# A 2x2 average pool whose first two tiles are loaded on two DMA queues

## The chip, the cores and the metric

The kernel runs on one core of a Trainium2 chip. The metric is the time of one execution on the device in microseconds (us), and where several runs were made, their median. The profile's span, from the first to the last of the program's instructions, is about 1.8 us shorter than that time.

## The reference, cut to what matters

```python
# x: (32, 128, 256, 256) float32; kernel_size = stride = 2; output (32, 128, 128, 128)
for i in range(h_out):
    for j in range(w_out):
        window = x[:, :, 2*i:2*i + 2, 2*j:2*j + 2]
        output[:, :, i, j] = np.mean(window, axis=(2, 3))
```

Each output is the mean of four inputs. 1073.74 MB come in, 268.44 MB go out, and there are three additions and a multiplication for each output.

## The kernel before

The work is cut into 128 tiles. A tile is 128 partitions with 32 units each, and a unit is two rows of an image (2 KB in, 512 B out). The first 127 tiles are alike; the last is loaded in parts of 16, 8 and 8 units, so that the end of the program can be handled in smaller pieces. There are two input buffers of 64 KB and three result buffers of 16 KB in each partition. SyncE issues the loads, VectorE adds rows and then columns, ScalarE multiplies by 0.25 and issues the stores.

```python
def tile_sums(b):                        # VectorE
    take(dve, stored[b], 16)             # the store of two tiles ago has left the result buffer
    take(dve, loaded[b], 16)             # the tile is there
    sums(ins[b], res[b], 2)              # rows, then columns in two halves

def scale_store(t, b, landed):           # ScalarE
    tile_scale(b, scaled)                # two halves; before the second one: free[b] += 1
    take(act, scaled, 2)
    act.dma_start(out=ot[t], in_=res[b]).then_inc(landed, 16)

load(0, 0)                               # SyncE: 8.389 MB each
load(1, 1)
# ... then for each tile t: take(sp, free[b]); load(t, b); at the end the three parts, and
for k, t in enumerate((whole - 2, whole - 1)):
    take(sp, held[k], 2)                 # the stores of the last two whole tiles go out
    sp.dma_start(out=ot[t], in_=res[t % 2]).then_inc(tail, 16)   # behind the last loads

# ScalarE: tile 0 apart from the loop, the others in it; the last two whole tiles:
for k, t in enumerate((whole - 2, whole - 1)):
    tile_scale(t % 2, held[k], frees=k == 0)
```

`take` waits for a semaphore and takes the amount off again. `held` tells SyncE that a result is ready for one of the last stores.

Of the kernel before, what the change touches and what calls it, by code (L numbers as in the profile page):

```python
# [9 lines left out]
@with_exitstack  # L10
def kernel(
    ctx: ExitStack,
    tc: tile.TileContext,
    x: bass.AP,
    kernel_size: bass.AP,
    stride: bass.AP,
    out: bass.AP,
):
    nc = tc.nc
    P = nc.NUM_PARTITIONS  # L20

    n, c, h, w = x.shape
    k = int(kernel_size)
    s = int(stride)
    h_out = (h - k) // s + 1
    w_out = (w - k) // s + 1
    R = n * c * h_out
    units = R // P if R % P == 0 else 0


    if k == 2 and s == 2 and h % 2 == 0 and w == 256 and units >= 1024:
        _pool_2x2(ctx, tc, x, out, units)
    else:
        _generic_pool(ctx, tc, x, out, k, s, n, c, h, w, h_out, w_out)


TILE = 32


def _pool_2x2(ctx, tc, x, out, units):  # L40
    nc = tc.nc
    P = nc.NUM_PARTITIONS
    f32 = mybir.dt.float32
    w = x.shape[3]
    w_out = w // 2
    sp, act, dve = nc.sync, nc.scalar, nc.vector

    xv = x.rearrange("n c (ho a) w -> (n c ho) (a w)", a=2)
    ov = out.rearrange("n c ho wo -> (n c ho) wo")


    in_pool = ctx.enter_context(tc.tile_pool(name="inp", bufs=2))
    out_pool = ctx.enter_context(tc.tile_pool(name="outp", bufs=3))
    ins = [in_pool.tile([P, TILE, 2 * w], f32, name="in_tile") for _ in range(2)]
    res = [out_pool.tile([P, TILE, w_out], f32, name="res") for _ in range(3)]

    def sem(name):
        return ctx.enter_context(nc.semaphore(name))

    loaded, free, stored = [[sem(f"{n}{b}") for b in range(2)] for n in ("loaded", "free", "stored")]  # L60
    halfway, summed, scaled, tail = [sem(n) for n in ("halfway", "summed", "scaled", "tail")]
    held = [sem(f"held{k}") for k in range(2)]



    def take(engine, sem, n=1):
        engine.wait_ge(sem, n)
        engine.sem_inc(sem, -n)  # L68

    def block(r0, g):  # L70
        rows = slice(r0, r0 + g * P)
        return xv[rows].rearrange("(p g) f -> p g f", p=P), ov[rows].rearrange("(p g) f -> p g f", p=P)

    whole, rest = divmod(units - 1, TILE)
    rest += 1
    xt = xv[0:whole * TILE * P].rearrange("(t p g) f -> t p g f", p=P, g=TILE)
    ot = ov[0:whole * TILE * P].rearrange("(t p g) f -> t p g f", p=P, g=TILE)
    parts, a = [], 0
    while a < rest:
        b = rest if rest - a <= 8 else a + (rest - a) // 2  # L80
        parts.append((a, b, sem(f"part{len(parts)}")))
        a = b



    def halves(pieces=2):
        if pieces == 1:
            return [slice(None)]
        return [slice(0, TILE // 2), slice(TILE // 2, TILE)]

    def load(t, b):
        sp.dma_start(out=ins[b], in_=xt[t]).then_inc(loaded[b], 16)

    def sums(it, dst, pieces=1):
        dve.tensor_add(out=it[:, :, 0:w], in0=it[:, :, 0:w], in1=it[:, :, w:]).then_inc(halfway)  # L95
        take(dve, halfway)
        for g in halves(pieces):
            dve.tensor_add(out=dst[:, g], in0=it[:, g, 0:w:2], in1=it[:, g, 1:w:2]).then_inc(summed)  # L98

    def tile_sums(b):  # L100
        take(dve, stored[b], 16)
        take(dve, loaded[b], 16)
        sums(ins[b], res[b], 2)

    def scale(dst, done=scaled):
        act.mul(out=dst, in_=dst, mul=0.25).then_inc(done)  # L106

    def tile_scale(b, done, frees=True):
        for k, g in enumerate(halves()):
            take(act, summed)  # L110
            if k and frees:
                act.sem_inc(free[b])
            scale(res[b][:, g], done)

    def scale_store(t, b, landed):
        tile_scale(b, scaled)
        take(act, scaled, 2)
        act.dma_start(out=ot[t], in_=res[b]).then_inc(landed, 16)

    with tc.tile_critical():  # L120

        load(0, 0)
        load(1, 1)
        pairs = (whole - 2) // 2
        with sp.Fori(2, 2 + 2 * pairs, 2) as i:
            for b in range(2):
                take(sp, free[b])
                load(i + b, b)
        for t in range(2 + 2 * pairs, whole):
            take(sp, free[t % 2])  # L130
            load(t, t % 2)



        take(sp, free[whole % 2])
        it, dst = ins[whole % 2], res[2]
        for a, b, part in parts:
            sp.dma_start(out=it[:, a:b], in_=block((whole * TILE + a) * P, b - a)[0]).then_inc(part, 16)
        for k, t in enumerate((whole - 2, whole - 1)):
            take(sp, held[k], 2)  # L140
            sp.dma_start(out=ot[t], in_=res[t % 2]).then_inc(tail, 16)


        for b in range(2):
            dve.sem_inc(stored[b], 16)
        with dve.Fori(0, whole // 2):
            for b in range(2):
                tile_sums(b)
        if whole % 2:
            tile_sums(0)  # L150
        for a, b, part in parts:
            take(dve, part, 16)
            sums(it[:, a:b], dst[:, a:b])


        scale_store(0, 0, stored[0])
        pairs = (whole - 3) // 2
        with act.Fori(1, 1 + 2 * pairs, 2) as i:
            for b in (1, 0):
                scale_store(i + 1 - b, b, stored[b])  # L160
        for t in range(1 + 2 * pairs, whole - 2):
            scale_store(t, t % 2, stored[t % 2])
        for k, t in enumerate((whole - 2, whole - 1)):
            tile_scale(t % 2, held[k], frees=k == 0)
        for a, b, _ in parts:
            take(act, summed)
            scale(dst[:, a:b])
            take(act, scaled)
            act.dma_start(out=block((whole * TILE + a) * P, b - a)[1], in_=dst[:, a:b]).then_inc(tail, 16)


    with tc.tile_critical():
        take(sp, tail, 16 * (len(parts) + 2))
# [95 lines left out]
```

## Time and profile before

| | before |
|---|---|
| median, lowest, highest (3 runs) | 3102.14, 3102.13, 3103.87 us |
| span of the profiled run | 3100.3 us |
| VectorE busy, ScalarE busy | 54%, 16% |
| load queue q1 and store queue q10, share of 16 DMA engines | 80.3%, 19.9% |
| moved over the span | 1342.19 MB, 433 GB/s |

The two shares of the DMA queues add up to the whole span, so the 16 DMA engines are the resource that is used up. The prediction shows the lines and reads them.

### The profile page before, as it was taken

To read this page: it belongs to the slowest core of one execution; us is meant where nothing else is said; L and a number is where in the kernel's file an instruction comes from. 1 tells how busy PE (TensorE), PEld (TensorE's weight loads), DVE (VectorE), ACT (ScalarE), POOL (GpSimd) and SP (SyncE) were. 2 spreads that over 40 slices of the span, in tenths; PEclk is the share of its full clock that TensorE was granted. 3 is DMA by queue.
4 is the path that set the end of the run, shared out by engine and by line. 5 is a ranking of instruction groups with operands and counts; after the bars stand their busy time and mean duration, and the time that the engine had idled before them with its cause. 6 is when DMAs were issued, how large, how long until landed. Compare 5 with 4: busy or idle time off the path is not lost. (4 is left out here: it accounts for less than half of the span.)

```text
span 3100.3 us, 2993 instructions
## 1 busy us (share of the span) xinstructions
DVE 1688.1 (54%) x387; ACT 490.3 (16%) x258; POOL 0.2 (0%) x4
## 2 busy tenths in 40 slices
DVE  4555555555555555555555555555555555555556
ACT  1111111111111111111111111111111111111111
POOL 0000000000000000000000000000000000000000
DMA  9999999999999999999999999999999999999999
GB/s 418 438 438 424 440 431 431 440 426 436 440 426 437 440 423 439 438 424 440 428 435 440 426 436 440 426 437 440 423 440 438 424 440 427 435 440 426 436 440 413
DMA packets 37440, 1342.19 MB, mean 433 GB/s; under 512 B 4160, under 2 KB 4160, under 8 KB 4416
## 3 DMA queue, kind: packets, MB, share of 16 engines
q1 hardware_dynamic: 19008, 1077.94, 80.3%
q10 hardware_dynamic: 18432, 264.25, 19.9%
HBM read 1073.74 MB, written 268.44 MB: 433 GB/s over the span
## 5 line engine op out<-in xcount | busy, mean ns | idle before, releaser
L95 DVE TENSOR_TENSOR in_tile<-in_tile 128x8192 f32<-128x8192 f32 (+1 forms) x130 | 1112.9, 8561 | 1385.7 <-DVEq L68 1385.7
L106 ACT ACTIVATE res<-res 128x2048 f32<-128x2048 f32 (+1 forms) x257 | 489.0, 1903 | 2569.5 <-ACTq L68 2569.5
L98 DVE TENSOR_TENSOR res<-in_tile 128x2048 f32<-128x2048 f32 (+1 forms) x257 | 575.4, 2280 | 19.0
L106 ACT ACT_TABLE_LOAD x1 | 1.3, 1283 | 34.3 <-ACTq L68 34.3
L250 POOL MEMSET const-bfloat16-1.0<- 128x1 bf16 x1 | 0.1, 101 | 0.0
L250 POOL MEMSET const-uint8-127<- 128x1 uint8 x1 | 0.1, 101 | 0.0
L250 POOL MEMSET const-float32-0.0<- 128x1 f32 x1 | 0.1, 98 | 0.2 <-issue 0.2
L250 POOL MEMSET const-float32-1.0<- 128x1 f32 x1 | 0.1, 98 | 0.0
## 6 DMA issues: line engine op xcount, KB each, us to landing
out_dram<-res ACTq DMA_DIRECT2D x125, 2048.0 KB, 32.5
in_tile<-in_x_dram SPq DMA_DIRECT2D x1, 4096.0 KB, 19.9
in_tile<-in_x_dram SPq DMA_DIRECT2D x2, 2048.0 KB, 26.6
out_dram<-res SPq DMA_DIRECT2D x2, 2048.0 KB, 23.7
in_tile<-in_x_dram SPq DMA_DIRECT2D x127, 34.3
out_dram<-res ACTq DMA_DIRECT2D x1, 1024.0 KB, 9.0
out_dram<-res ACTq DMA_DIRECT2D x2, 512.0 KB, 6.3
```

Of the source, the lines that this page charges most:

```text
L95: dve.tensor_add(out=it[:, :, 0:w], in0=it[:, :, 0:w], in1=it[:, :, w:]).then_inc(halfway)
L98: dve.tensor_add(out=dst[:, g], in0=it[:, g, 0:w:2], in1=it[:, g, 1:w:2]).then_inc(summed)
L106: act.mul(out=dst, in_=dst, mul=0.25).then_inc(done)
L250: nc = _bacc.Bacc("TRN2", target_bir_lowering=False, num_devices=1)
```

## The change

The intent is to start both queues at once. In the trace of the kernel before, the store queue has nothing to do until the first store is issued at 39.42 us, so it takes a quarter of each of the first two tiles. GpSimd joins the two halves of a load into the one semaphore that VectorE waits for. A dummy activation is to bring the load of ScalarE's table forward, which comes at 34.31 us in that trace. Two smaller edits come along: the last two whole tiles are scaled in one piece instead of two halves, and the first tile is now in ScalarE's loop.

```diff
+SIDE = 8
...
-    held = [sem(f"held{k}") for k in range(2)]
+    held, begun = [[sem(f"{n}{k}") for k in range(2)] for n in ("held", "begun")]
...
-        load(0, 0)
-        load(1, 1)
+        for b in range(2):
+            for engine, g in ((sp, slice(0, TILE - SIDE)), (act, slice(TILE - SIDE, TILE))):
+                engine.dma_start(out=ins[b][:, g], in_=xt[b][:, g]).then_inc(begun[b], 16)
+            take(nc.gpsimd, begun[b], 32)
+            nc.gpsimd.sem_inc(loaded[b], 16)
...
-            take(sp, held[k], 2)
+            take(sp, held[k])
...
-        scale_store(0, 0, stored[0])
-        pairs = (whole - 3) // 2
-        with act.Fori(1, 1 + 2 * pairs, 2) as i:
+        act.mul(out=scratch, in_=nc.const_aps.tensor(0.0, [P, 1], f32), mul=0.25)
+        pairs = (whole - 2) // 2
+        with act.Fori(0, 2 * pairs, 2) as i:
...
-            tile_scale(t % 2, held[k], frees=k == 0)
+            take(act, summed, 2)
+            if k == 0:
+                act.sem_inc(free[t % 2])
+            scale(res[t % 2], held[k])
```

More of the change, by code (lines that the diff above doesn't have):

```diff
@@ L55, in _pool_2x2 @@
     res = [out_pool.tile([P, TILE, w_out], f32, name="res") for _ in range(3)]
+    scratch = ctx.enter_context(tc.tile_pool(name="scratch", bufs=1)).tile([P, 1], f32, name="scratch")
     def sem(name):
@@ L106, in scale, with scale_store @@
         act.mul(out=dst, in_=dst, mul=0.25).then_inc(done)
-    def tile_scale(b, done, frees=True):
+    def scale_store(t, b, landed):
         for k, g in enumerate(halves()):
             take(act, summed)
-            if k and frees:
+            if k:
                 act.sem_inc(free[b])
-            scale(res[b][:, g], done)
-    def scale_store(t, b, landed):
-        tile_scale(b, scaled)
+            scale(res[b][:, g])
         take(act, scaled, 2)
@@ L153, in _pool_2x2 @@
             sums(it[:, a:b], dst[:, a:b])
-        scale_store(0, 0, stored[0])
-        pairs = (whole - 3) // 2
-        with act.Fori(1, 1 + 2 * pairs, 2) as i:
-            for b in (1, 0):
-                scale_store(i + 1 - b, b, stored[b])
-        for t in range(1 + 2 * pairs, whole - 2):
+        act.mul(out=scratch, in_=nc.const_aps.tensor(0.0, [P, 1], f32), mul=0.25)
+        pairs = (whole - 2) // 2
+        with act.Fori(0, 2 * pairs, 2) as i:
+            for b in range(2):
+                scale_store(i + b, b, stored[b])
+        for t in range(2 * pairs, whole - 2):
             scale_store(t, t % 2, stored[t % 2])
         for k, t in enumerate((whole - 2, whole - 1)):
-            tile_scale(t % 2, held[k], frees=k == 0)
+            take(act, summed, 2)
+            if k == 0:
+                act.sem_inc(free[t % 2])
+            scale(res[t % 2], held[k])
         for a, b, _ in parts:
```

## The prediction

> **What bounds the kernel now.** I read the page of the kernel before in this order: the busy time of the engines, the slices with their DMA shares, the DMA queues. Then I asked the trace for stretches of ten tiles in the middle, for the timeline at both ends and for the waits.
>
> ```profile
> span 3100.3 us, 2993 instructions
> DVE 1688.1 (54%) x387; ACT 490.3 (16%) x258; POOL 0.2 (0%) x4
> DMA  9999999999999999999999999999999999999999
> q1 hardware_dynamic: 19008, 1077.94, 80.3%
> q10 hardware_dynamic: 18432, 264.25, 19.9%
> HBM read 1073.74 MB, written 268.44 MB: 433 GB/s over the span
> ```
>
> The busiest compute engine works 54% of the span, while the packets of the two DMA queues (q1 is the load queue of SyncE, q10 the store queue of ScalarE) fill 80.3% + 19.9% = 100.2% of the time of the 16 DMA engines. So the bound is the transfer of 1342.19 MB, and the question for any change is: does it remove bytes (this one does not), does it raise the rate, or does it remove time in which the engines have no packet? The middle gives the rate. In the windows of the middle the columns are DVE, ACT and POOL busy, the TensorE clock (unused here), the DMA share and GB/s.
>
> ```profile
> 300.00:542.00 242.00, 131.86 (x30) 38.39 (x21) 0.00 (x0) 1.00 1.00 433
> 2000.00:2242.00 242.00, 131.85 (x30) 38.20 (x20) 0.00 (x0) 1.00 1.00 434
> ```
>
> Ten tiles take 242 us and the DMA share is 1.00. More exactly, the timeline starts the first sum of tile 3 at 91.31 us and that of tile 125 at 3041.47 us, so one tile takes (3041.47 - 91.31) / 122 = 24.18 us. A tile is 8.389 MB in and 2.097 MB out, 10.486 MB, which makes 433.6 GB/s. The packet records of the trace fit: an engine moves one partition's 64 KB in 2.418 us and one partition's 16 KB of a store in 0.605 us, and eight of each per tile make 8 x 3.023 = 24.18 us. The program is 128 such tiles (127 and a last one in three parts): 128 x 24.18 = **3095.2 us** at the steady rate. That leaves 3100.3 - 3095.2 = 5.1 us for everything the change could touch at the two ends. The timeline shows where they are.
>
> ```profile
> 0.95 0.87 SPq L92 DMA_DIRECT2D in_tile<-in_x_dram  x2
> 23.07 8.69 DVE L95 TENSOR_TENSOR in_tile<-in_tile 128x8192 f32<-128x8192 f32 x1 [23.07 <-DVEq L68]
> 34.31 1.28 ACT L106 ACT_TABLE_LOAD   x1 [34.31 <-ACTq L68]
> 36.80 0.34 SPq L92 DMA_DIRECT2D in_tile<-in_x_dram  x1
> 39.42 0.39 ACTq L118 DMA_DIRECT2D out_dram<-res  x1
> 42.41 8.69 DVE L95 TENSOR_TENSOR in_tile<-in_tile 128x8192 f32<-128x8192 f32 x1 [6.00 <-DVEq L68]
> 3094.17 0.34 ACTq L169 DMA_DIRECT2D out_dram<-res  x1
> ```
>
> The first packet starts at 2.02 us and the last ends at 3098.99 us in the packet records, a stretch of 3096.97 us. So the 5.1 us split into 2.02 us before the first packet, 3096.97 - 3095.2 = 1.8 us of imperfect filling in between, and 1.3 us after the last packet (its completion and the closing barrier). Counting the packets in flight, I find 16 of 16 engines holding a packet in every half microsecond from 3.0 to about 3098, including the two places where one would look for a hole: around 41 us, between the second load and the third, and from 3065 us on, where the last parts are summed. What the eye takes for a loss at the start (DVE idle for 23 us, then 6.00 us before the second tile) is idle time of an engine that is not the bottleneck. It costs nothing: the second tile landed 42.41 - 23.07 = 19.34 us after the first, and 8.389 MB in 19.34 us is 433.7 GB/s, so **one queue alone already ran at the full rate**.
>
> [...] loads alone from one queue ran at 433.7 GB/s, loads and stores from two at 433.6 GB/s. [...] The trace shows that alternation from the first store on: one 64 KB packet, one 16 KB packet. [...]
>
> **The change part by part.**
>
> 1. *Splitting the first two loads.* Each tile was 8 packets of 64 KB on each engine; it becomes 8 of 48 KB from the load queue and 8 of 16 KB from the store queue. The bytes are the same: 8 x (1.814 + 0.605) = 8 x 2.418 = 19.35 us, with the 48 KB packet taken as three quarters of the measured 64 KB one. If the two queues take turns, tile 0 still lands near 22.9 us and tile 1 19.35 us later. The store queue is otherwise empty until 39.42 us, so nothing is displaced. Gain or loss on the path: 0. The four issues cost ScalarE some 0.4 us each (0.393 and 0.425 us on SyncE), beside an idle engine. Both issuers leave the opening barrier at about 0.8 us, so the first packet still starts near 2.0 us. The fill of the first packets (they took 3.1 to 3.4 us in place of 2.42, about 0.7 us) stays, for it is the first latency of each engine whatever the queue.
>
> 2. *The relay through GpSimd.* It waits for both halves and adds to the semaphore that VectorE waits on. A hop of that kind (ScalarE's wait, its increment, SyncE's wait met) runs from 36.49 to 36.60 us in this trace, so 0.1 to 0.2 us more on tile 0 and tile 1, and then nothing. It lies beside the transfer of tile 1, thus 0 on the end.
>
> 3. *The dummy activation.* It moves the 1.28 us table load from 34.31 us to about 2 us, where ScalarE is idle. The scale of the first half begins 1.28 us earlier; the second half still waits for its sum (about 36.5 us) and starts near 36.6 in place of 37.4, so the first store is issued about 0.9 us earlier, at some 38.5 us. The engines are still moving tile 1 until 41.4 us, so the store only joins the queue earlier. Stores begin up to one round (0.6 us of transfer per engine) sooner, and the loads then land that much later: an exchange inside a saturated stream, 0 on the end.
>
> 4. *The third load* is issued when tile 0's second sum is picked up, 36.80 us, against an end of tile 1 at 41.4 us. Even with the relay's 0.2 us, the queue is fed about 4 us ahead. In steady state the next load is issued about 13.7 us after a tile lands, with 24.18 us of work, of which about 10 us are left in the queue.
>
> 5. *The last two whole tiles scale in one piece.* One activation of 4096 elements: two halves took 1.91 us each, so I estimate 3.7 us, starting when both sums are there. The held store of tile 125 moves from 3056.99 to about 3058.8 us, that of tile 126 from 3081.1 to about 3082.9 us. Both go to the end of a load queue that holds earlier work: the store of tile 125 landed 32.6 us after its issue, at 3089.6 us, so the one behind it needs to be in the queue only by about 3088. Cost 0. The first part's scale starts at 3085.87 us, after the longer activation is over.
>
> 6. *The tail.* The last store is issued at 3094.17 us and needs about 1.2 us of transfer at 433 GB/s, yet the engines work until 3098.99: there are about 2.5 us of backlog to absorb a VectorE chain that comes later by the 0.6 us of part 3.
>
> Sum: 0 on the rate, 0 on the bytes, between -1 and +0.5 us at the ends. I take -0.3 us, mostly for the third load's first packets, which took 2.5 to 2.8 us and may come back to 2.42 once the store's start no longer falls on them.
>
> **The rivals.** *(a) The two-queue start fills the engines better.* If the first latencies of two queues overlap, the 0.7 us of fill shrinks, and with it perhaps the bubble of the third load. For it: the two together are most of the 1.8 us. Against it: both queues run on the same 16 engines[...]. It would make 3100.5 to 3101.2 us. *(b) A new hole.* ScalarE's issues come late, tile 0's last 16 KB pieces wait behind 48 KB packets of tile 1, and the third load comes after tile 1 has ended. One such packet is 1.8 us, the feed is 4 us ahead, so two would be needed before anything shows: 3102 to 3105 us. *(c) A shifted tail.* The later held stores or the later VectorE chain outrun the 2.5 us of backlog: 3102.5 to 3104 us. *(d) The phase of the two queues changes for good,* and 127 tiles each gain or lose. [...] a loss would need a queue to run dry each round, against 10 us of lead. I hold it for very unlikely.
>
> **Range and chances.** The time before is 3102.14 us with one run of three at 3103.87, a spread of 1.7 us that is larger than the effect. I predict 3101.8 us. Rival (a) sets the lower end at 3100.2; rivals (b) and (c) and the chance that the median falls on the higher value set the upper end at 3103.9. Two per cent are 62 us, twelve times all the time that is not steady transfer, so within 2% is all but certain: 0.985, faster 0.005, slower 0.01.
>
> **What would show it right or wrong.** In the profile after: the middle windows still at 242 us per ten tiles; VectorE's first start at 22.9 to 23.4 us and its second 19.3 to 19.5 us later (a first start above 24.5 speaks for (b)); the table load before 3 us and the first store issued near 38.5 us; a last store issue between 3093.5 and 3095.5 us with packets still in flight for some 4 us after it. A change of span above 2 us with the same middle would say that an end holds a hole I have not seen; a change of the middle would make my main step, a saturated stream, wrong.

Of its support "0 on the rate" keeps the measured rates, 433.7 GB/s by one queue and 433.6 by two; that the rate cannot rise was not shown. The sum came to 0 on the rate, 0 on the bytes and -0.3 us at the ends, from 3102.14 to 3101.8 us.

## The result

| | before | after |
|---|---|---|
| median | 3102.14 us | 3102.44 us |
| lowest to highest (6 runs each) | 3101.94 to 3103.87 us | 3102.23 to 3103.82 us |
| span of the profiled run | 3100.3 us | 3100.6 us |

The ratio is 1.000 with a 95% interval from 0.9987 to 1.0013, which is about 4 us either way. Ratios in this document are those of the runs of one kernel to those of the kernel before in the same rounds; they are not quite the ratio of the medians. The change made no difference that could be measured.

These are the page's lines of the kernel after that answer to those of before: the span, the busy times, the DMA shares in 40 slices, the two queues.

```profile
span 3100.6 us, 2999 instructions
DVE 1688.1 (54%) x387; ACT 490.2 (16%) x257; POOL 0.2 (0%) x4
DMA  9999999999999999999999999999999999999999
q1 hardware_dynamic: 19008, 1073.75, 79.9%
q10 hardware_dynamic: 18720, 268.44, 20.2%
```

Some bytes went from q1 to q10: q10 grew from 264.25 to 268.44 MB, which is the 2 x 2.097 MB of the pieces. The sum of the shares is 100.1%, against 100.2% before. The windows in the middle (DVE, ACT and POOL busy, TensorE clock, DMA share, GB/s) are as they were:

```profile
300.00:542.00 242.00, 131.86 (x30) 38.40 (x21) 0.00 (x0) 1.00 1.00 433
2000.00:2242.00 242.00, 131.85 (x30) 38.19 (x20) 0.00 (x0) 1.00 1.00 434
```

The timeline at both ends after (start, duration, engine, line, operation, what it waited for):

```profile
0.91 0.89 ACTq L125 DMA_DIRECT2D in_tile<-in_x_dram  x2
0.95 0.87 SPq L125 DMA_DIRECT2D in_tile<-in_x_dram  x2
1.83 1.28 ACT L163 ACT_TABLE_LOAD   x1 [1.83 <-issue]
...
23.34 8.69 DVE L98 TENSOR_TENSOR in_tile<-in_tile 128x8192 f32<-128x8192 f32 x1 [23.34 <-DVEq L71]
...
37.07 19.73 SPq L95 DMA_DIRECT2D in_tile<-in_x_dram  x2
39.02 0.37 ACTq L118 DMA_DIRECT2D out_dram<-res  x1
42.77 8.69 DVE L98 TENSOR_TENSOR in_tile<-in_tile 128x8192 f32<-128x8192 f32 x1 [6.09 <-DVEq L71]
...
3094.26 0.34 ACTq L179 DMA_DIRECT2D out_dram<-res  x1
```

The new issues on ScalarE's queue and the early table load are there. VectorE starts the first tile at 23.34 us instead of 23.07, the second 19.43 us later instead of 19.34. The first store is issued at 39.02 us, 0.40 us earlier, and the last one at 3094.26 us, 0.09 us later. In the packet records the first packet starts at 1.95 us (1.97 before) and the last ends at 3099.09 us (3098.94 before). Everything that was moved is visible; the last packet ends 0.15 us later, and the span is 0.3 us longer.

### The profile page after: what moved, and what is told of

Its sections match the earlier page's. It is cut to its first block, busy times and chain, and to the rows that moved or that the text cites. A ratio compares the mean times of both kernels' runs of the same rounds, so it can differ in the third digit from the quotient of the medians. Undisturbed runs are those within 1.5% of the kernel's fastest.

```text
span 3100.6 us, 2999 instructions
## 1 busy us (share of the span) xinstructions
DVE 1688.1 (54%) x387; ACT 490.2 (16%) x257; POOL 0.2 (0%) x4
## 3 DMA queue, kind: packets, MB, share of 16 engines
q10 hardware_dynamic: 18720, 268.44, 20.2%
HBM read 1073.74 MB, written 268.44 MB: 433 GB/s over the span
## 5 line engine op out<-in xcount | busy, mean ns | idle before, releaser
L109 ACT ACTIVATE res<-res 128x2048 f32<-128x2048 f32 x255 | 488.7, 1916 | 2602.1 <-ACTq L71 2602.1
```

What stands on the lines that cost most here:

```text
L109: act.mul(out=dst, in_=dst, mul=0.25).then_inc(done)
```

## The experiments

The theory: the DMA engines are full from the first packet to nearly the last, so only bytes and holes in their work count, and each part of the change lies beside that work. The rivals: the change is a gain and a loss that cancel; the idle store queue at the start was free room; every delay of the start or the tail adds to the end. Twelve kernels ran, all with correct results. The calls ran on different chips, so each kernel is compared with the runs of the kernel before of its own call. Code cuts are shortened where `...`, `as` or a remark in brackets stands. Three numbers help in reading them: an engine moves one partition's 64 KB in 2.418 us, a tile takes 24.18 us, and 2.097 MB at 433.6 GB/s take 4.84 us.

### The parts one by one

`split_only` is the kernel before with the two-queue start alone (the first hunks of the diff above).

> The kernel before with only the two-queue start (and the GpSimd relay). Theory (saturated engines): same time as before, 3101.5 to 3103 us, within 1 us of it; first VectorE start near 23.3 us. Rival (the change is a gain and a loss that cancel): the split alone gains 0.7 to 1.8 us, so about 3100.5 to 3101.4 us.

`dummy_only` is the kernel before with the early activation alone.

```diff
+        act.mul(out=scratch, in_=nc.const_aps.tensor(0.0, [P, 1], f32), mul=0.25)
         scale_store(0, 0, stored[0])
```

> The kernel before with only the early dummy activation. Theory: same time, 3101.5 to 3103 us; table load near 1 us, the first store issued near 38.5 us, 0.9 us earlier than before, with no effect on the end. Rival (an earlier first store shortens the run): 0.9 us less.

`one_piece_only` is the kernel before with the last hunk of the diff and `take(sp, held[k])`.

> The kernel before with only the one-piece scale of the last two whole tiles. Theory: same time, 3101.5 to 3103 us, although the held stores are issued 1.8 us later. Rival (cancelling parts): the later held stores cost 1 to 1.8 us, so 3103 to 3104 us in the median.

`after_no_split` is the changed kernel with `load(0, 0)` and `load(1, 1)` put back.

> The changed kernel with the first two loads put back on the load queue alone. Theory: same time, 3101.5 to 3103 us. Rival (cancelling parts): without the split's gain it comes out 0.7 to 1.8 us slower than before.

They ran on one chip, in five rounds, beside nine runs of the kernel before (median 3102.16 us):

| kernel | median | ratio (95% interval) |
|---|---|---|
| split_only | 3102.48 us | 1.0002 (0.9989 to 1.0016) |
| dummy_only | 3101.95 us | 0.9998 (0.9985 to 1.0012) |
| one_piece_only | 3102.09 us | 1.0000 (0.9987 to 1.0014) |
| after_no_split | 3102.43 us | 1.0001 (0.9987 to 1.0015) |

All four medians lie within 0.4 us of the kernel before. No gain of 0.7 us or more appears in the split alone, and no loss when it is taken out again, so the rival of cancelling parts has no support; the intervals of about 4 us do not exclude it by themselves. The traces narrow it down: in the packet records the stretch from the first packet to the end of the last is 3096.97 us before, 3097.15 us after, 3097.25 us in `split_only`, 3096.79 us in `dummy_only` and 3097.06 us in `after_no_split` (one profiled run each; that of `one_piece_only` was disturbed, as shown below). No part is worth more than about 0.3 us there; smaller effects stay open. The timeline of `dummy_only`:

```profile
0.91 1.28 ACT L158 ACT_TABLE_LOAD   x1 [0.91 <-SPq L122]
...
38.48 0.39 ACTq L120 DMA_DIRECT2D out_dram<-res  x1
...
3094.00 0.34 ACTq L172 DMA_DIRECT2D out_dram<-res  x1
```

The first store is issued 0.94 us before that of the kernel before (39.42 us), as worked out. Little of that lead reaches the engines: the first packet of a store starts at 43.90 us in place of 44.01. The last store is issued 0.17 us earlier.

### More bytes at the start

If the store queue's idle time at the start were free room, a load put there would cost nothing. `extra_store_queue` adds 2.097 MB to the changed kernel, into the result buffer that is used only at the end. In this test and the next two VectorE also waits for the extra load before it sums the last tile (not shown).

```diff
             for engine, g in ((sp, slice(0, TILE - SIDE)), (act, slice(TILE - SIDE, TILE))):
                 engine.dma_start(out=ins[b][:, g], in_=xt[b][:, g]).then_inc(begun[b], 16)
+            if b == 0:
+                act.dma_start(out=res[2] as [P, 8, 512], in_=xt[0][:, 0:8]).then_inc(extra, 16)
             take(nc.gpsimd, begun[b], 32)
```

> The changed kernel with 2.097 MB more, loaded into the idle result buffer of the last tile, on the store queue between its two early pieces. Theory (all 16 engines already full while the store queue is empty): 2.097 MB / 433.6 GB/s = 4.84 us longer, 3106.5 to 3108 us. Rival (the store queue idles for the first 41 us, and work put there is free): no longer than before, 3101.5 to 3103.5 us.

It was 3121.49 us, ratio 1.0060 (1.0043 to 1.0077), some 18.6 us longer (0.0060 x 3103). Neither number was right. The timeline and the windows of this run show why:

```profile
23.34 8.69 DVE L100 TENSOR_TENSOR in_tile<-in_tile 128x8192 f32<-128x8192 f32 x1 [23.34 <-DVEq L73]
67.67 8.69 DVE L100 TENSOR_TENSOR in_tile<-in_tile 128x8192 f32<-128x8192 f32 x1 [31.00 <-DVEq L73]
```

```profile
70.00:75.00 5.00, 5.00 (x1) 0.00 (x0) 0.00 (x0) 1.00 0.26 111
75.00:80.00 5.00, 4.85 (x3) 1.08 (x1) 0.00 (x0) 1.00 0.00 0
80.00:85.00 5.00, 5.00 (x2) 2.74 (x2) 0.00 (x0) 1.00 0.62 210
```

The second tile arrives 44.33 us after the first. Its piece on the store queue stood behind the extra load. When its turn came, the load queue was already on the third tile, so each 16 KB packet of the piece waited for a 64 KB packet (2.42 us), and eight such rounds of 3.02 us are 24 us. The buffer of tile 1 thus came free late, the fourth load was issued late, and the engines stood empty from 71.6 to 82.3 us (DMA share 0.00 in the middle window). The 4.84 us of bytes and the 10.7 us of hole make 15.5 us. One engine also ended 1.5 us after the others. Summed over the packet records, packets took 2.3 us per engine longer than in the changed kernel, nearly all of it from 60 us on. Together that is 19.3 us; the profiled run is 19.0 us longer than that of the changed kernel (spans of 3119.6 and 3100.6 us). The test failed as a test of the rival and showed something more useful: here the two queues took turns, and a piece of 2.097 MB, 4.84 us by its own bytes, took the 24 us of eight rounds beside the 64 KB packets.

`extra_load_queue` puts the same extra load into the kernel before, on the load queue between its first two loads.

```diff
         load(0, 0)
+        sp.dma_start(out=res[2] as [P, 8, 512], in_=xt[0][:, 0:8]).then_inc(extra, 16)
         load(1, 1)
```

> The kernel before with the same 2.097 MB more, on the load queue between its two first loads. Theory: 4.84 us longer again, the same as on the other queue, 3106.5 to 3108 us. Rival (the queue matters): dearer here than on the store queue by more than 1.5 us.

3108.49 us, ratio 1.0017 (1.0000 to 1.0033), or 5.3 us. The difference is as expected; the median lies 0.5 us above the range named, which was set for a kernel before at 3102 us, while that had 3103.40 us in this call.

`extra_behind_nothing` repeats the failed test where nothing waits behind the extra load.

```diff
+        act.dma_start(out=res[2] as [P, 8, 512], in_=xt[0][:, 0:8]).then_inc(extra, 16)
         scale_store(0, 0, stored[0])
```

> The kernel before with the same 2.097 MB more, on the store queue at the very start, with no piece of a tile behind it. In the first test of this kind the extra load delayed a piece of tile 1 in the same queue and the engines then stood empty from 71.6 to 82.3 us; here nothing waits for it. Theory (the engines are full while the store queue is empty): first VectorE start 4.84 us later, near 27.9 us, and the run 4.84 us longer than before, 3106.5 to 3109 us (an engine that falls behind by 2 us, seen in slower runs, included). Rival (room in the idle store queue): same first start, 3101.5 to 3103.5 us.

```profile
0.91 0.40 ACTq L159 DMA_DIRECT2D res<-in_x_dram  x1
...
28.06 8.69 DVE L97 TENSOR_TENSOR in_tile<-in_tile 128x8192 f32<-128x8192 f32 x1 [28.06 <-DVEq L70]
```

3107.01 us, ratio 1.0015 (1.0001 to 1.0028), or 4.7 us, and the first tile arrives 4.99 us later than before. All five runs lie above all nine of the kernel before, and the spans of the profiled runs differ by 4.9 us (3105.2 against 3100.3). So the load on the idle store queue at 0.91 us was paid for at its full transfer time of 4.84 us, on that queue (4.7 us) as on the other (5.3 us). **Here the idle queue was not idle bandwidth.** The rival of free room falls.

### Delays and holes at the start

`start_late_short` and `start_late_long` let GpSimd write zeros before it passes on the news of tile 0, once 128x1536 and four times 128x4096.

```diff
             take(nc.gpsimd, begun[b], 32)
+            if b == 0:
+                for _ in range(1):      # start_late_long: range(4) and res[2][:, 0:32]
+                    nc.gpsimd.memset(res[2][:, 0:12], 0.0).then_inc(lag)
+                    take(nc.gpsimd, lag)
             nc.gpsimd.sem_inc(loaded[b], 16)
```

> The changed kernel with GpSimd holding back the news of tile 0 by one memset of 128x1536 (its length D is read from the profile[...]). Theory: the third load has about 3.3 us to spare (issued 37.07 us, about 1 us to its first packet, tile 1's packets end at 41.3 to 41.9 us), so D below 3.3 us costs nothing: 3101.5 to 3103 us. Rival (every delay of the start chain adds to the end): longer by D.

> As start_late_short with four memsets of 128x4096[...]. Theory: the excess over the spare time becomes a hole in the engines and is paid in full: longer by D - 3.3 us. Rivals: longer by D (no spare time at all), or not longer (the hole is made up later).

The short delay was D = 25.00 - 23.34 = 1.66 us by VectorE's first start; the time was 3103.78 us, ratio 1.0002 (0.9985 to 1.0019). By the times alone this is inconclusive: all four runs lie at 3103.3 to 3104.0, but so do four of the seven runs of the kernel before in that call (median 3103.40 us). The packet records show no common hole: fifteen engines take up the third tile between 41.4 and 42.0 us, nearly as in the kernel after (41.2 to 41.9 us), and one does so at 42.6 us. That one engine then stays behind, so it is open whether the delay cost something there. The long delay was D = 37.97 - 23.34 = 14.63 us; 3115.85 us, ratio 1.0041 (1.0025 to 1.0058), or 12.7 us, where the theory wanted D - 3.3 = 11.3 us and the rival of no spare time 14.6 us. The interval, 8 to 18 us, excludes only that the hole is made up; the trace decides between the other two. Its timeline and windows:

```profile
37.97 8.69 DVE L100 TENSOR_TENSOR in_tile<-in_tile 128x8192 f32<-128x8192 f32 x1 [37.97 <-DVEq L73]
51.70 45.56 SPq L97 DMA_DIRECT2D in_tile<-in_x_dram  x3
```

```profile
30.00:40.00 10.00, 2.03 (x1) 0.00 (x0) 7.39 (x3) 1.00 1.06 459
40.00:45.00 5.00, 5.00 (x1) 0.00 (x0) 0.00 (x0) 1.00 0.03 10
45.00:50.00 5.00, 4.85 (x3) 0.77 (x1) 0.00 (x0) 1.00 0.00 0
```

The engines are empty from about 41.7 us, when tile 1 is done, until the third load's first packet at 52.7 us, 1.0 us after its issue at 51.70 us. That hole of 11.0 us is 3.6 us less than D, which is the spare time of the start chain. It is paid in full and never made up. Most of the first packets after it took 2.9 to 3.3 us in place of 2.42, and one engine fell 1.3 us behind; 11.0 + 0.7 + 1.3 = 13.0 us. The profiled run is 13.6 us longer than that of the changed kernel (3114.2 against 3100.6 us), so some 0.6 us are left open.

`tile_per_queue` keeps both queues busy at the start, but with a whole tile on each.

```diff
+        load(0, 0)
+        act.dma_start(out=ins[1], in_=xt[1]).then_inc(loaded[1], 16)
-        (the two-queue start with its relay)
```

> The changed kernel with the first tile whole on the load queue and the second whole on the store queue, so that the two share the engines packet by packet. Theory: both land near 42 us, the third load is issued near 42.4 + 13.7 = 56 us, and the engines are empty from about 42 to 57 us: 15 us longer, about 3117.5 us. Rival (only bytes count, the order in which the tiles land doesn't): same time, 3101.5 to 3103 us.

3120.16 us, ratio 1.0059 (1.0042 to 1.0075), or 18.3 us, where 15 us were expected. This timeline starts with VectorE's first work:

```profile
42.61 8.69 DVE L98 TENSOR_TENSOR in_tile<-in_tile 128x8192 f32<-128x8192 f32 x1 [42.61 <-DVEq L71]
51.45 4.49 DVE L101 TENSOR_TENSOR res<-in_tile 128x2048 f32<-128x2048 f32 x2
55.86 8.68 DVE L98 TENSOR_TENSOR in_tile<-in_tile 128x8192 f32<-128x8192 f32 x1
```

Both tiles land together at 42.6 us, and the engines are empty from about 41.7 to 57.3 us. So the same bytes on the same two queues cost 15.6 us of hole when the tiles become whole in another order. The profiled runs differ by 17.7 us (3118.3 against 3100.6): in the packet records, packets took 1.4 us per engine longer than in the kernel after, and the last engines ended some 0.6 us behind the others. The kernel after, in which both queues carry tile 0 first and tile 1 second, has no such hole: VectorE starts tile 0 at 23.34 us, the third load is issued at 37.07 us, and the engines take it up from 41.2 to 41.9 us, as tile 1 ends.

### Delays in the tail

`tail_late_short` and `tail_late_long` give VectorE more work before the last part: one sum of 128x2048, or two of 128x4096, in a buffer that is no longer needed.

```diff
             take(dve, part, 16)
+            if b == rest:               # tail_late_long: 0:16, then the same for 16:32
+                dve.tensor_add(out=ins[0][:, 0:8, 0:w], in0=ins[0][:, 0:8, 0:w], in1=ins[0][:, 0:8, w:]).then_inc(halfway)
+                take(dve, halfway)
             sums(it[:, a:b], dst[:, a:b])
```

> The changed kernel with one more VectorE sum of 128x2048 (2.28 us) before the last part. Theory: the last store is issued 2.3 us later (about 3096.5 us), and the engines' backlog of about 2.6 us absorbs it: 3101.5 to 3103.5 us. Rival (the chain VectorE, ScalarE, last store sets the end): 2.3 us longer, about 3104.7 us.

> As tail_late_short with two sums of 128x4096 (8.8 us). Theory: 8.8 - 2.6 = 6.2 us longer, about 3108.6 us. Rivals: 8.8 us longer, 3111.2 us (no backlog), or no longer (the tail hides more).

The short one has a median of 3103.07 us, ratio 1.0001 (0.9984 to 1.0018): two runs at 3102.2 and 3102.3 us, two at 3103.8 and 3103.9, where the rival wanted 2.3 us more in each. The profiled run is one of the latter two. In it the last whole tile already arrived 1.5 us late; its last store was issued at 3098.24 us, 3.98 us later than in the kernel after, and its last packet ended 1.51 us later (3100.60 us), so 2.47 us were absorbed. The long one is at 3109.42 us, ratio 1.0024 (1.0007 to 1.0040), or 7.4 us, where 6.2 us were expected. By the times alone (2 to 12 us) the rival of 8.8 us is not excluded. Its last store, and the DMA part of its stretch from 3088 to 3108 us (40 slices of 0.5 us):

```profile
3103.44 0.34 ACTq L184 DMA_DIRECT2D out_dram<-res  x1
```

```profile
GB/s 459 459 360 328 524 459 492 295 492 360 459 360 442 426 360 492 336 418 344 33 0 0 0 0 0 0 0 0 0 0 0 0 188 418 410 33 0 0 0 0
```

The engines run out of work near 3097.5 us and start again for the last store. That store is issued 3103.44 - 3094.26 = 9.18 us later than in the kernel after, while the last packet ends 6.62 us later (3105.71 against 3099.09): 2.56 us of the delay were absorbed. The profiled run itself (3109.10 us) is 6.7 us above the median of the kernel after; the slower of the four runs make the 7.4.

### Where the two levels of the times come from

The runs of the kernel before, of the kernel after and of most kernels that cost nothing fall on two levels, near 3102.2 and near 3103.9 us (`dummy_only` has five on the lower one, `start_late_short` four on the upper one). The profile of `one_piece_only` caught a run of the upper level (3104.07 us, span 3102.3 us). From its stretch 3096 to 3102 us, 40 slices of 0.15 us:

```profile
DMA  9699999999999999962000000000000000000000
GB/s 410 273 464 410 464 410 382 382 437 382 437 410 464 410 437 382 410 246 82 27 27 27 27 27 27 27 27 27 27 0 27 27 27 0 0 0 0 0 0 0
```

At the end the rate is not 433 but 27 GB/s: that is one engine of sixteen (433.6 / 16 = 27.1), which alone still moves its share for some 2 us while the other fifteen have no packet. The landing records show since when. I took, for each tile, the time between the last but one and the last engine to finish its load. From the fourth tile on it is 2.07 us in this run. It reaches 1.3 to 1.5 us in the profiled run of `start_late_short` (3103.97 us) and 0.9 us late in that of `tail_late_short` (3103.94 us), where the last engine is 1.5 us behind the middle one. In the five profiled runs of the lower level (before, after and the other three parts) it is 0.22 us or less from there on. So in the profiled runs the upper level goes with one engine that falls behind and does not catch up; the fifteen that were done did not take over its rows. In `one_piece_only` and `start_late_short` this comes about while the third and fourth tiles are loaded, in `tail_late_short` mostly in the second half of the run. Why one falls behind in some runs is open.

## Why the prediction was right

**The saturated stream** (its main step) held. The middle windows did not change, and the three tests with changed order or bytes were paid in transfer time and holes: 4.7 to 5.3 us for 4.84 us of bytes, 12.7 us for a hole of 11.0 us and what came after it. Two readings of the packets need correcting: its times of the first and the last packet are 0.05 us late (1.97 and 3098.94 us in the trace; the stretch is right), and the 16 KB packets stand in the records with 0.611 us, not 0.605; the latter is what they add to a round of 3.022 us.

**Part 1, the split,** held: tile 1 followed tile 0 by 19.43 us, inside the 19.3 to 19.5 us given, and the fill of the first packets stayed: an engine's first 48 KB and 16 KB packets took 3.08 us together in the mean, where its first 64 KB packet took 3.19 us before and a later one 2.42, and tile 0's data had landed at 22.52 us against 22.59. ScalarE issues two of the four pieces, in 0.89 us together. Rival (a) hoped to overlap it; the stretch from the first packet to the end of the last was 3097.15 us against 3096.97.

**Part 2, the relay,** was sized about right, and lay beside the path as said. From the last landing of tile 0 among the packets to its first sum 0.82 us passed in place of 0.48, which is 0.34 us more. The relay is 0.13 us of that, inside the 0.1 to 0.2: from the last landing in the semaphore records to the first sum it took 0.27 us (23.076 to 23.342) in place of 0.14 (22.939 to 23.075). The other 0.21 us passed before that last landing; their cause is not shown. The first sum began only 0.27 us later than before, within the range given for it, since the data had landed 0.07 us sooner.

**Part 3** was right about the end and off in a size. The first store came at 39.02 us, not 38.5. `dummy_only` has 38.48 us, so the activation does what was said. In the changed kernel the first sum begins 0.41 us later than in `dummy_only`, of which the relay is 0.13 us, and this store is in the loop, whose address instructions before the issue take 0.14 us (38.88 to 39.02 us). Stores were also not a round sooner among the packets: the first one starts at 43.94 us, against 44.01 before.

**Part 4,** "the queue is fed about 4 us ahead", measured 3.6 us in `start_late_long`.

**Parts 5 and 6** held: one activation of 4096 elements took 3.62 us (estimate 3.7), the held store left at 3058.75 us (3058.8), and the backlog of "about 2.5 us" absorbed 2.56 us in `tail_late_long` and 2.47 us in `tail_late_short`.

**The sum** had the wrong sign: -0.3 us was predicted, and the medians differ by +0.3 us. Neither can be told from zero in an interval of 4 us. The expected recovery of the third load's first packets was small: they took 2.42 to 2.71 us instead of 2.5 to 2.8, and 2.78 to 2.89 us in `split_only`, so it is no steady effect of the change. That the median came so close to the forecast was in part luck, since the two levels are 1.7 us apart and the forecast had no cause for them.

**Rival (b) was mis-sized.** It counted a badly placed piece as 1.8 us and the damage as 3 us at most. The change keeps clear of it, but `extra_store_queue` and `tile_per_queue` show that the wrong order in two queues cost some 14 us beside the extra bytes in the one and 18 us in the other, since in the one the piece took eight rounds beside the other queue (24 us), and in both the late buffer then opened a hole (10.7 and 15.6 us).

## What to carry to other kernels

Where the shares of the DMA queues add up to the whole span, compute first how much time is not steady transfer; here it was 5.1 us of 3100, and as long as the steady rate stays as it is, no rearrangement of queues could be worth more. Here a second queue added no bandwidth to engines that were full (tile 1 followed tile 0 by 19.43 us on two queues, by 19.34 us on one), but a second order of arrival, which was neutral in the change and opened holes of 10.7 and 15.6 us in two tests, so give both queues the pieces of the tile that is needed first. When a few microseconds are in dispute, delay a chain on purpose and read off how much the end absorbs: that gives the spare time as a number.
